# A five-pair block in Down, and a last pair that multiplies with tokens stationary onto transposed accumulators

## The chip, the cores and the metric

The kernel runs on one core of one Trainium2 chip. The metric is the device time of one execution, in microseconds (us). Five engines work side by side and wait for each other through semaphores: TensorE (PE; PEld is its weight load), VectorE (DVE), ScalarE (ACT), GpSimd (POOL) and SyncE (SP), whose queue starts most of the DMAs. Matmul results go to PSUM, which has eight banks of 128 partitions by 512 fp32 values; DVE and ACT read them from there.

## The reference

One step of a transformer layer over 576 tokens that matter to the output (512 prompt rows and 64 sample rows) with 2048 features. After attention, the part that the change touches is:

```python
h = rmsnorm(x, lp['norm_ffn_g'])
x = x + (jax.nn.silu(h @ lp['ffn_w_gate']) * (h @ lp['ffn_w_up'])) @ lp['ffn_w_down']
...
y_prompt = rmsnorm(xp[:, N_META:], final_norm_g)
y_sample = rmsnorm(xs, final_norm_g)
```

The hidden width is 5632, so that Down (`@ ffn_w_down`) sums over 44 rows of 128 hidden features, taken as 22 pairs. `rmsnorm` divides each token by the root of the mean of its squared features and multiplies each feature by its gain.

## The kernel before

All activations lie transposed: features on partitions, tokens along the free dimension (576 tokens, in two halves of `QH` = 288). Every fp32 value is split in two fp32r parts, a high one (copied by ACT) and a low one (the rest, subtracted by DVE, L157 and L154), and a product is three matmuls: high by high, high by low, low by high.

Gate, up and most of Down run as a scheme of seven products instead of eight (`winograd`): two 128-row blocks of weights and two token halves make a 2 by 2 problem; sums and differences of the weight quarters are formed on POOL and DVE (L1220), those of the token quarters once per pair (`G.tensor_tensor` at the end of each gate-and-up turn), and each of the seven results is added into up to two quarters.

The gate-and-up loop goes over `u` = 0 to 21. At its end pair `u` of the hidden activations is spilled to DRAM (`opspill`) by `spill_operands`, whose steps are taken one at a time between the products of the following turns: first the four plain quarters as high and low part, then, for pairs that Down takes in seven products, the four differences as well. The high parts pass through one staging tile, tag `s`, with a single buffer (`squad`).

Down takes the pairs in blocks: `blocks = [4, 4, 4, 4, 4, 2]`. In each of the first five, for each of eight groups of 256 output columns (`d`), `down_rows` loads 1024 rows of weights (`fetch_raw`, two buffers, requested ahead), splits them product by product and runs 7 products of 12 matmuls with 288 columns (weights stationary, tokens streaming, lines L1234 and L1238). DVE adds each product into the accumulators `y[0..15]` in SBUF (L1500). Operands of the next block are loaded by `builder`, one per product (`step`). Each pair has one of eight slots, `m % 8`: seven tiles `b1_s` to `b7_s`.

The last block, pairs 20 and 21, is plain: `plain_rows` runs 24 matmuls for each token half and column group, loading and splitting the weights once for each half. `squares` then squares each y half on POOL or ACT, sums over column groups on POOL (L1521, L1524), and multiplies y by the final gain on ACT (L1525). `finish(h)` sums over partitions with small matmuls against ones (L1552), forms the reciprocal root (`rsqrt`, L166 to L170), turns y into token rows by transposes on PE (L1538), scales them on the way out of PSUM (L1568, L1570) and stores them. `finish` of the first half is interleaved with the second half's matmuls.

The program is written as one order; the compiler places each engine's instructions by readiness and by that order, except where `keep_in_program_order` binds them. Each engine and the SP queue then run what they have in strict order.

Of the kernel before, what the change touches and what calls it, by code (L numbers as in the profile page):

```python
# [116 lines left out]
def encoder_step(  # L117
# [32 lines left out]
    def f32(ap):  # L150
        return ap.bitcast(F32)
# [167 lines left out]
    with ExitStack() as ph:  # L319
# [223 lines left out]

        rows = 39
        gT = cp.tile([P, rows], F32, name="gT")
        gF, gE, gq, gkv, g08 = (gT[:, a:b] for a, b in ((0, 16), (16, 32), (32, 36), (36, 38), (38, 39)))

# [86 lines left out]
        def projections():  # L634
# [20 lines left out]
            def bias_table():  # L655
# [8 lines left out]
                row = 0  # L664
                for g in (g_ffn, g_fin, g_q, g_kv, g_sub):
# [687 lines left out]

    def builder(m0, count, plain, by_product=False):

        places = {1: 0, 2: 1, 4: 2, 5: 3} if plain else {1: 0, 2: 2, 3: 3, 5: 4, 6: 5, 4: 6, 7: 7}
        todo = [(m, p) for m in range(m0, m0 + count) for p in places]
        if by_product:
            order = [p for p, _ in CHAIN]
            todo.sort(key=lambda mp: order.index(mp[1]))  # L1360
        for m, p in todo:
            hl = bc.tile([P, 2, QH], F32R, name=f"b{p}_{m % 8}")
            load(f32(hl), opspill[m, :, places[p]])
            operands[m % 8, p] = hl[:, 0], hl[:, 1]
            yield

    def spill_operands(m, parts):
# [26 lines left out]

    blocks = [4, 4, 4, 4, 4, 2]

# [17 lines left out]
    start = builder(0, blocks[0], False, True)  # L1414
    for u in range(FC // 2):
# [56 lines left out]

    def plain_rows(m0, n, d, hs, slots, done):

        banks = {(f, h): pmt()[:, 0:QH] for f in range(2) for h in hs}
        r = fetched.pop((m0, d, hs))
        for g in range(0, n, 2):
            wh = fw.tile([P, 2, 4, P], F32R, name="wh", tag="wh", bufs=2)
            wl = fw.tile([P, 2, 4, P], F32R, name="wl", tag="wl", bufs=2)
            for f in range(2):  # L1480
                split(wh[:, f], wl[:, f], r[:, 2 * g:2 * g + 4, f * P:(f + 1) * P])
                for k in range(4):
                    m = slots[g + k // 2]
                    ops = [operands[m, ((1, 2), (4, 5))[k % 2][h]] for h in hs]
                    mm3([banks[f, h] for h in hs], wh[:, f, k], wl[:, f, k], [o[0] for o in ops],
                        [o[1] for o in ops], g + k == 0, g + k == n + 1)
        for f in range(2):
            for h in hs:
                c = y[2 * d + f][:, h * QH:(h + 1) * QH]
                V.tensor_tensor(c, c, banks[f, h], op=ALU.add)  # L1490
                done(2 * d + f, h)

    def down_rows(m0, n, d, slots, step):
# [10 lines left out]

    tok = [[(0, NS), (NS, P), (192, 96)], [(QH, P), (416, P), (544, 32)]]
    sqs = {}
    LATE = 2
    s4 = squad()

    def squares(i, h):  # L1510
        c = y[i][:, h * QH:(h + 1) * QH]
        if h and i >= KC - LATE:
            sqs[h, i] = s4[:, 2 + i % 2]
            S.activation(sqs[h, i], c, AF.Square)
        elif i == 0:
            sqs[h] = s4[:, h]
            G.tensor_tensor(sqs[h], c, c, op=ALU.mult)
        else:
            t = s4[:, 2 + i % 2]
            if h or i % 2 == 0:  # L1520
                G.tensor_tensor(t, c, c, op=ALU.mult)  # L1521
            else:
                S.activation(t, c, AF.Square)  # L1523
            G.tensor_tensor(sqs[h], sqs[h], t, op=ALU.add)  # L1524
        S.activation(c, c, AF.Copy, scale=gE[:, i:i + 1])  # L1525

    def finish(h, ahead):

        groups = [(q, j) for q in range(4) for j in range(3)]

        def turned(q, j):
            o, n = tok[h][j]
            ps = pmt()
            for k in range(4):
                PE.transpose(ps[0:n, k * P:(k + 1) * P], y[q * 4 + k][:, o:o + n], ident)  # L1538
            return ps

        held = []
        for g in groups[:ahead]:
            held.append(turned(*g))
            yield
        pc = pmt()
        vc = yy.tile([P, 3], F32, name=f"vc{h}")
        rc = yy.tile([P, 3], F32, name=f"rc{h}")
        V.memset(vc, 1.0)
        for j, (o, n) in enumerate(tok[h]):
            parts = [sqs[h]] + [sqs[h, i] for i in range(KC - LATE, KC) if h]  # L1550
            for q in parts:
                PE.matmul(pc[0:n, 2 * j:2 * j + 2], q[:, o - h * QH:o - h * QH + n], ones[:, 0:2],  # L1552
                          start=q is parts[0], stop=q is parts[-1])
            V.tensor_scalar(vc[0:n, j:j + 1], pc[0:n, 2 * j:2 * j + 1], 1.0 / D, EPS, op0=ALU.mult, op1=ALU.add)
        rsqrt(rc, vc)
        yield
        for i, (q, j) in enumerate(groups):
            o, n = tok[h][j]
            ps = held.pop(0) if held else turned(q, j)
            k = i - i // 3  # L1560
            if h and i % 3 < 2:
                if k % 4 == 0:
                    four = fd.tile([P, 4, 512], F32, name="ot", tag="raw", bufs=2)
                ot = four[:, k % 4]
            else:
                ot = yy.tile([P, 4, P], F32, name="ot", tag="ws", bufs=3).rearrange("p a b -> p (a b)")
            if i % 2:
                S.activation(ot[0:n], ps[0:n, :], AF.Copy, scale=rc[0:n, j:j + 1])  # L1568
            else:
                V.tensor_scalar(ot[0:n], ps[0:n, :], rc[0:n, j:j + 1], None, op0=ALU.mult)  # L1570
            cs = slice(q * 512, (q + 1) * 512)
            out_queue = G.dma_start if h and i in (1, 3, 4, 7) else store
            if o == 0:
                out_queue(y_sample[:, cs], ot[0:NS])
            else:
                out_queue(y_prompt[o - NS:o - NS + n, cs], ot[0:n])
            yield

    wanted, m0 = [], 0
    for bi, n in enumerate(blocks):  # L1580
        last = bi + 1 == len(blocks)
        wanted += [(m0, d, (h,)) for h in range(2) for d in range(KC // 2)] if last else [(m0, d) for d in range(KC // 2)]
        m0 += n
# [3 lines left out]
    def fetch_raw():  # L1587
        if wanted:
            key = wanted.pop(0)
            fetched[key] = load_raw(fd, w_down, key[0] * 256, 2 * sizes[key[0]], key[1] * 256, 2)  # L1590

    fetch_raw()
    for _ in start:
        pass
    first = 0
    for bi, n in enumerate(blocks):
        slots = [(first + k) % 8 for k in range(n)]
        if bi + 1 < len(blocks):
            build = builder(first + n, blocks[bi + 1], bi + 2 == len(blocks))

# [5 lines left out]
            for d in range(KC // 2):  # L1606
                if bi == 0 and d + 1 < KC // 2:
                    load_y(d + 1)
                down_rows(first, n, d, slots, step)
                fetch_raw()  # L1610
                if bi + d == 0:
                    for _ in spilling:
                        pass
                    close_rw()
                    yy, close_yy = pool("yy", "right")
            for _ in build:
                pass
        else:
            before = iter(())
            tc.keep_in_program_order(S.preload_act_table_set("natural_log_exp_and_others"))  # L1620
            for h in range(2):
                for d in range(KC // 2):
                    plain_rows(first, n, d, (h,), slots, squares)
                    fetch_raw()
                    for _ in range(min(d, 2)):
                        next(before, None)
                before = finish(h, 5 * h)
            for _ in before:
                pass
        first += n  # L1630
    close_yy()
    close_fd()
    close_fc()
# [68 lines left out]
```

## Time and profile before

| | us |
|---|---|
| median of 3 runs (lowest, highest) | 2421.4 (2421.13, 2422.16) |
| span of the profiled execution | 2421.5 |
| attention and projections | to about 888 |
| gate and up | about 888 to 1879 |
| Down, five blocks of seven products | about 1879 to 2340.3 |
| two plain pairs, norm, output | 2340.3 to 2421.5 |

The profiled execution's own time lies among the three runs; its span is within 0.1 us of their median. In the profile a group of instructions is named by its line, its engine and what it writes from what. Busy time of PE includes overlap of matmuls in flight, so the price of a matmul is read from start to start of its successors, not from its duration. Windows give the busy time of each engine in a stretch, then the granted clock of PE (PEclk), the busy share of the DMA engines, and GB/s.

### The profile page before, as it was taken

To read this page: it belongs to the slowest core of one execution; us is meant where nothing else is said; L and a number is where in the kernel's file an instruction comes from. 1 tells how busy PE (TensorE), PEld (TensorE's weight loads), DVE (VectorE), ACT (ScalarE), POOL (GpSimd) and SP (SyncE) were. 2 spreads that over 40 slices of the span, in tenths; PEclk is the share of its full clock that TensorE was granted. 3 is DMA by queue.
4 is the path that set the end of the run, shared out by engine and by line. 5 is a ranking of instruction groups with operands and counts; after the bars stand their busy time and mean duration, and the time that the engine had idled before them with its cause. 6 is when DMAs were issued, how large, how long until landed. Compare 5 with 4: busy or idle time off the path is not lost. (4 is left out here: it accounts for less than half of the span.)

```text
span 2421.5 us, 44043 instructions
## 1 busy us (share of the span) xinstructions
PE 2362.1 (98%) x17472; PEld 2324.8 (96%) x17472; DVE 1897.9 (78%) x2781; ACT 1134.4 (47%) x2005; POOL 778.4 (32%) x514
## 2 busy tenths in 40 slices
PE   7999999999999999999999999999999999999998
PEld 6999999999998999999999999999999999999997
DVE  5666677676674789888888888898887888888875
ACT  5445555444443554444444444444444433333345
POOL 1100000130000456554554654555554222222235
PEclk9999999999999999999999999999999999999999
DMA  7433333253323643445444444544446873663434
GB/s 220 141 100 88 91 86 95 73 172 103 114 89 127 183 147 130 134 145 164 141 140 156 157 130 149 164 133 142 161 153 222 304 259 111 217 219 102 135 105 149
DMA packets 362886, 354.21 MB, mean 146 GB/s; under 512 B 23970, under 2 KB 320568, under 8 KB 362680
## 3 DMA queue, kind: packets, MB, share of 16 engines
q1 hardware_dynamic: 360694, 345.76, 45.4%
q0 software_dynamic: 1648, 5.12, 0.7%
q8 instruction: 137, 2.24, 0.4%
q14 instruction: 69, 0.57, 0.1%
q10 hardware_dynamic: 338, 0.52, 0.1%
HBM read 271.09 MB, written 81.16 MB: 145 GB/s over the span
## 5 line engine op out<-in xcount | busy, mean ns | idle before, releaser
L1234 PE MATMUL m<-b,wh 128*128 128x288 f32 x7168 | 1046.2, 295 | 1.9 <-ACT wh L157 1.9
L1234 PEld LDWEIGHTS m<-b,wh 128*128 128x128 f32 x7168 | 982.8, 188 | 3.2 <-ACT wh L157 2.7
L1238 PE MATMUL m<-b,wl 128*128 128x288 f32 x3584 | 582.8, 298 | 6.3 <-DVE wl L154 3.0
L154 DVE TENSOR_TENSOR wl<-raw,wh 128x1024 fp32r<-128x1024 f32 (+1 forms) x379 | 530.8, 1404 | 55.3 <-ACT wh L157 55.0
L1238 PEld LDWEIGHTS m<-b,wl 128*128 128x128 f32 x3584 | 511.4, 188 | 16.3 <-DVE wl L154 16.2
L157 ACT ACTIVATE wh<-raw 128x1024 fp32r<-128x1024 f32 (+1 forms) x379 | 329.7, 874 | 377.9 <-PE m L1234 326.3
L1220 POOL TENSOR_TENSOR ws<-raw 128x512 f32<-128x512 f32 (+1 forms) x124 | 219.7, 1772 | 607.2 <-DVE wl L154 351.8
L157 ACT ACTIVATE wh<-ws 128x512 fp32r<-128x512 f32 (+1 forms) x248 | 193.4, 780 | 280.2 <-DVE wl L154 118.8
L154 DVE TENSOR_TENSOR wl<-ws,wh 128x512 fp32r<-128x512 f32 (+1 forms) x248 | 247.4, 998 | 5.1 <-ACT wh L157 4.6
L109 PE MATMUL ps<-xh,wh 128*128 128x296 f32 (+1 forms) x992 | 223.6, 307 | 2.1 <-DVE ls L586 1.2
L109 PE MATMUL ps<-xl,wh 128*128 128x296 f32 (+1 forms) x992 | 215.9, 299 | 0.5 <-DVE xl L162 0.5
L109 PE MATMUL ps<-xh,wl 128*128 128x296 f32 (+1 forms) x960 | 208.0, 298 | 0.0
L1374 DVE TENSOR_TENSOR c<-c,s 128x288 fp32r<-128x288 f32 x168 | 166.4, 990 | 0.0
L109 PEld LDWEIGHTS ps<-xh,wh 128*128 128x128 f32 x992 | 160.6, 190 | 4.7 <-ACT wh L157 1.4
L109 PEld LDWEIGHTS ps<-xl,wh 128*128 128x128 f32 x992 | 161.5, 190 | 0.9 <-DVE xl L162 0.9
L1500 DVE TENSOR_TENSOR y<-y,m 128x288 f32<-128x288 f32 x280 | 125.7, 449 | 40.9 <-PE m L1238 40.8
L109 PEld LDWEIGHTS ps<-xh,wl 128*128 128x128 f32 x960 | 156.1, 190 | 0.0
L1220 POOL TENSOR_TENSOR raw<-raw 128x1024 f32<-128x1024 f32 (+1 forms) x46 | 143.2, 3113 | 3.5
L157 ACT ACTIVATE wh<-wr 128x1024 fp32r<-128x1024 f32 (+1 forms) x110 | 101.7, 924 | 88.2 <-PE ps L109 59.5
L1330 DVE TENSOR_TENSOR c<-c,m 128x288 f32<-128x288 f32 x171 | 73.2, 449 | 88.7 <-PE m L1238 51.5
L154 DVE TENSOR_TENSOR wl<-wr,wh 128x1024 fp32r<-128x1024 f32 (+1 forms) x108 | 116.0, 1074 | 28.0 <-ACT wh L157 25.9
L1393 POOL TENSOR_TENSOR c<-c,rb 128x576 f32<-128x576 f32 x44 | 79.0, 1795 | 139.2 <-ACT c L1392 139.2
(368 smaller groups left out, 3164.3 us busy)
## 6 DMA issues: line engine op xcount, KB each, us to landing
raw<-in_ffn_w_gate SPq DMA_DIRECT2D x44, 1024.0 KB, 9.2
raw<-in_ffn_w_up SPq DMA_DIRECT2D x44, 1024.0 KB, 6.9
b<-opspill SPq DMA_DIRECT2D x148, 288.0 KB, 6.0
raw<-in_ffn_w_down SPq DMA_DIRECT2D x40, 1024.0 KB, 5.7
wr<-in_w_in SPq DMA_DIRECT2D x57, 512.0 KB, 4.0
opspill<-s SPq DMA_DIRECT2D x42, 576.0 KB, 3.1
opspill<-c SPq DMA_DIRECT2D x42, 576.0 KB, 6.3
wr<-in_w_out SPq DMA_DIRECT2D x16, 512.0 KB, 4.3
```

Of the source, the lines that this page charges most:

```text
L109: self.tc.keep_in_program_order(self.pe.matmul(out, lhsT, rhs, start=start, stop=stop))
L154: V.tensor_tensor(lo, src, f32(hi), op=ALU.subtract)
L157: S.activation(hi, src, AF.Copy)
L1220: (G if p in (5, 7) else V).tensor_tensor(x, y, z, op=ALU.add if p == 5 else ALU.subtract)
L1234: PE.matmul(banks[p], wh[:, k, :], x, start=first and new and k == 0 and x is hi, stop=False, skip_group_check=not new)
L1238: PE.matmul(banks[p], wl[:, k, :], hi, start=False, stop=last and k == n - 1, skip_group_check=not new)
L1330: V.tensor_tensor(c, c, banks[p], op=ALU.add)
L1374: V.tensor_tensor(src[:, k].bitcast(F32R), src[:, k], f32(hi[:, k]), op=ALU.subtract))
L1393: G.tensor_tensor(g[:, f, :], g[:, f, :], rb2, op=ALU.mult)
L1500: V.tensor_tensor(c, c, banks[p], op=ALU.add)
```

## The change

`blocks` becomes `[4, 4, 4, 4, 5, 1]`.

The fifth block takes five pairs in seven products (15 matmuls a product). Pair 20 is therefore spilled with its differences (the test `u < FC // 2 - blocks[-1]` now lets it through). Its seven operands share slot 4 with pair 12 of the fourth block; `builder` asks for them in the fourth block's last column group, one behind each product. A load of weight rows has up to 1280 rows; its two buffers become one in each of two pools (`fd`, `fe`). Two of the accumulators, y13 and y14, move to the buffer of tag `s`.

The last pair, 21, runs the other way round. `last_operands` loads its plain quarters as four tiles of 576 tokens and its 256 rows of weights as eight tiles of 512 columns, and splits these, all during the fifth block and into slots 5 to 7. `last_rows` then goes over five token tiles (four of 128 prompt tokens, one of 64 sample tokens) and four groups of 512 columns: four transposes lay y into a bank as token rows, and six matmuls (two hidden blocks by three parts, tokens stationary, 512 weight columns streaming) add the last pair onto it. ACT squares the bank with a sum along the row and copies it out; the reciprocal root is formed per token tile; DVE multiplies by it and by the gain, which is loaded as rows on all partitions; the tile is stored. The transposed gain `gE`, `plain_rows`, `squares` and `finish` go.

```diff
-        rows = 39
+        rows = 23
...
-    blocks = [4, 4, 4, 4, 4, 2]
+    blocks = [4, 4, 4, 4, 5, 1]
...
+        if count > 4:
+            for _ in range(49 - len(todo)):
+                yield
+            for p in order:
+                fetch_operand(m0 + 4, p)
+                yield
...
-            y.update((i, yy.tile([P, TQ], F32, name=f"y{i}")) for i in range(13, KC))
+            y2 = fr.tile([P, 2, TQ], F32, name="y", tag="s", bufs=1)
+            y[13], y[14] = y2[:, 0], y2[:, 1]
+            y[15] = yy.tile([P, TQ], F32, name="y15")
...
+    def last_operands():
+
+        for f in range(2):
+            for s in range(2):
+                t = bc.tile([P, 2, QH], F32R, name="lt", tag=spare.pop(0))
+                load(f32(t), opspill[last_m, :, 2 * f:2 * f + 2, s])
+                tokens[f, s] = t.rearrange("p a b -> p (a b)")
+                yield
+        raws = {}
+        for c in range(4):
+            for f in range(2):
+                raws[f, c] = bc.tile([P, 512], F32, name="lr", tag=spare[2 * c + f])
+                r0 = (2 * last_m + f) * P
+                load(raws[f, c], w_down[r0:r0 + P, c * 512:(c + 1) * 512])
+                yield
+        turn = spare[8:] + spare[:8]
+        for c in range(4):
+            for f in range(2):
+                hi, lo = (bc.tile([P, 512], F32R, name=n, tag=turn.pop(0)) for n in ("lh", "ll"))
+                split(hi, lo, raws[f, c])
+                w_last[f, c] = hi, lo
+                yield
+                yield
...
+            for c in range(4):
+                bank = pmt()[0:n]
+                for k in range(4):
+                    PE.matmul(bank[:, k * P:(k + 1) * P], y[4 * c + k][:, o:o + n], ident, is_transpose=True,
+                              start=k == 0, stop=False)
+                for f in range(2):
+                    for t, s in ((0, 0), (1, 0), (0, 1)):
+                        PE.matmul(bank, tokens[f, t][:, o:o + n], w_last[f, c][s], start=False,
+                                  stop=f == 1 and s == 1)
+                x, junk = chunk("lx"), chunk("lj")
+                S.activation(junk[0:n], bank, AF.Square, accum_out=ssq[0:n, c:c + 1])
+                S.activation(x[0:n], bank, AF.Copy)
+                if final:
+                    V.tensor_tensor(x[0:n], x[0:n], gains[c][0:n], op=ALU.mult)
+                xs.append(x)
+            v = yy.tile([P, 1], F32, name="v", bufs=2)
+            r = yy.tile([P, 1], F32, name="r", bufs=2)
+            V.reduce_sum(v[0:n], ssq[0:n], axis=AX.X)
+            V.tensor_scalar(v[0:n], v[0:n], 1.0 / D, EPS, op0=ALU.mult, op1=ALU.add)
+            rsqrt(r[0:n], v[0:n])
+            for c, x in enumerate(xs):
+                cs = slice(c * 512, (c + 1) * 512)
+                if not final:
+                    V.scalar_tensor_tensor(x, x, r, gains[c], op0=ALU.mult, op1=ALU.mult)
+                    store(rows[:, cs], x)
+                elif c < 2:
+                    V.tensor_scalar(x[0:n], x[0:n], r[0:n], None, op0=ALU.mult)
+                    store(rows[:, cs], x[0:n])
+                else:
+                    S.activation(x[0:n], x[0:n], AF.Copy, scale=r[0:n])
+                    S.dma_start(rows[:, cs], x[0:n])
...
-            build = builder(first + n, blocks[bi + 1], bi + 2 == len(blocks))
+            build = last_operands() if bi + 2 == len(blocks) else builder(first + n, blocks[bi + 1])
...
+                    other, close_other = pool("fe")
+                    into.insert(0, other)
+                fetch_raw()
```

More of the change, by code (lines that the diff above doesn't have):

```diff
@@ L1471, in encoder_step @@
     fd, close_fd = pool("fd")
[L1473 to L1491, printed above, removed]
     def down_rows(m0, n, d, slots, step):
@@ L1527, in finish @@
[L1527 to L1577, printed above, removed]
@@ L1579, in encoder_step @@
     wanted, m0 = [], 0
-    for bi, n in enumerate(blocks):
-        last = bi + 1 == len(blocks)
-        wanted += [(m0, d, (h,)) for h in range(2) for d in range(KC // 2)] if last else [(m0, d) for d in range(KC // 2)]
+    for n in blocks[:-1]:
+        wanted += [(m0, d) for d in range(KC // 2)]
         m0 += n
@@ L1618, in encoder_step @@
         else:
-            before = iter(())
             tc.keep_in_program_order(S.preload_act_table_set("natural_log_exp_and_others"))
[L1621 to L1629, printed above, removed]
+            last_rows()
         first += n
     close_yy()
+    close_other()
     close_fd()
```

65 lines of the change are left out of this document (33 added, 32 removed).

## The prediction

> **What bounds the kernel now.** I read the page first, then the busy times by stage, then the order of PE's instructions in Down and at the end.
>
> ```profile
> PE 2362.1 (98%) x17472; PEld 2324.8 (96%) x17472; DVE 1897.9 (78%) x2781; ACT 1134.4 (47%) x2005; POOL 778.4 (32%) x514
> ```
>
> ```profile
> core 0: us, PE busy (x) PEld busy (x) DVE busy (x) ACT busy (x) POOL busy (x), PEclk, DMA share, GB/s
> ...
> 1859.20:1880.70 21.50, 21.50 (x164) 21.50 (x163) 11.87 (x13) 8.48 (x14) 8.58 (x6) 1.00 1.06 387
> 1880.70:1900.00 19.30, 17.66 (x129) 16.99 (x129) 17.91 (x34) 8.14 (x14) 4.73 (x4) 1.00 1.03 341
> 2248.70:2340.30 91.60, 91.04 (x674) 89.48 (x674) 80.19 (x129) 36.73 (x58) 18.63 (x14) 1.00 0.31 95
> 2340.30:2380.10 39.80, 36.58 (x256) 33.86 (x255) 23.46 (x46) 24.68 (x50) 24.69 (x30) 1.00 0.49 155
> 2380.10:2404.00 23.90, 23.90 (x177) 23.86 (x178) 18.43 (x29) 12.88 (x26) 16.45 (x21) 0.93 0.46 142
> 2404.00:2421.50 17.50, 8.29 (x76) 7.16 (x73) 6.18 (x14) 6.17 (x13) 2.20 (x4) 0.89 0.51 169
> ```
>
> TensorE is the bound nearly everywhere, so a change counts by the PE time that it removes, plus what it does to the few stretches where PE waits. The fifth Down block lasts from 2248.7 to 2340.3. Behind it stand 81.2 us (to 2421.5): the two plain pairs with the turned output between them, and a drain in which PE is busy for 8.3 of 17.5 us. All that is replaced lies in these last two stretches; the two rows ahead of them are the entry into Down, where the change adds a spill.
>
> **Price of a matmul.** The timeline at the end of the fifth block:
>
> ```profile
> 2338.18 0.70 PE L1238 MATMUL m<-b,wl 128*128 128x288 f32 x4
> 2338.72 1.22 PE L1234 MATMUL m<-b,wh 128*128 128x288 f32 x8
> 2339.77 0.70 PE L1238 MATMUL m<-b,wl 128*128 128x288 f32 x4
> ```
>
> Twelve matmuls of 288 columns from 2338.18 to 2339.77: 0.1328 us each, start to start. The new last pair streams 512 columns instead; the nearest rows stand in the attention:
>
> ```profile
> 613.43 0.40 PE L109 MATMUL po<-pk0l,vh 128*128 128x512 f32 x1
> 613.67 0.40 PE L109 MATMUL po<-pk0h,vl 128*128 128x512 f32 x1
> 613.90 0.34 PE L109 MATMUL sp<-kmh,qnh 128*128 128x400 f32 x1
> ```
>
> That is 0.24 and 0.23, so 0.235 us each. The Trainium skill, page "TensorE: Matmul & The Clock Gate", section "Back-to-back issue gap", gives N/2.4 + 2.5 ns for a lone stream, 216 ns at 512 columns; by it the 120 matmuls below would take 25.9 us instead of 28.2. The rows here, each with its own weight load, are slower, and I go by them.
>
> The chain of waits gives the transposes and the present end:
>
> ```profile
> 2400.08 0.87 PE m L1538 x8
> 2400.96 3.18 PE m L185 x24
> 2404.14 3.06 PE m L1538 x28
> ...
> 2409.68 0.21 ACT rc L166
> ...
> 2411.41 0.74 DVE ot L1570
> ...
> 2414.99 0.68 ACT ot L1568
> ```
>
> A transpose costs 0.109 us (28 in 3.06, 8 in 0.87), and going from matmuls to transposes and back costs nothing beside (0.87 and then 3.18 for 24 at 0.1325).
>
> **The change, part by part.**
>
> *The fifth block with five pairs.* It had 8 x 84 = 672 matmuls, 89.2 us; it lasts 91.6, so 2.4 us are stalls, about 0.3 at each of the seven changes of columns. It gets 8 x 105 = 840 matmuls, 111.6 us. I keep the 2.4 us (0 at best, 1.25 times at worst): 114.0, ending at 2362.7. DVE decides whether more is lost:
>
> ```profile
> L154 DVE TENSOR_TENSOR wl<-raw,wh 128x512 fp32r<-128x512 f32 x22 | 22.2, 1007 | 0.0
> L1500 DVE TENSOR_TENSOR y<-y,m 128x288 f32<-128x288 f32 x49 | 22.0, 449 | 6.8 <-PE m L1238 6.8
> ```
>
> Of DVE's 80.2 us in the block, 56 additions into y take 25.1 and stay the same; the other 55.1 grow by 5/4. That is 94.0 us of 114. The last pair's eight splits, which move into this block, add 8 x 1.0 = 8, still 12 us under PE. But they are asked for within three columns (43 us), where DVE then has 35.3 + 8: full. Price between 0 and about 4 us (half of the splits uncovered); I take 0, because the splits are needed only after the block and the products' own splits stand ahead of them.
>
> *Fetching the fifth pair.* Its seven operands go into slot 4, which the fourth block still reads in its last columns; each can be loaded only after its product. The plain pairs load into slots 4 and 5 at the same border now:
>
> ```profile
> 2238.60 5.65 SPq L138 DMA_DIRECT2D b<-opspill  x6
> 2248.16 0.38 SPq L138 DMA_DIRECT2D raw<-in_ffn_w_down  x1
> ```
>
> ```profile
> b<-opspill SPq DMA_DIRECT2D x148, 288.0 KB, 6.0
> ```
>
> Columns take 11.5 us (91.6/8), so the loads start 1.4 us into the last columns, right after the first product, and 10 us ahead of the border at 2248.7. One lands after 6 us and is wanted 1.1 us past the border at the earliest (eight matmuls of the other four pairs): it costs nothing. Each load holds SP for about 0.9 us (5.65/6); behind it stand weight rows for the columns after the next, with 14 us of room, and the last pair's own loads, wanted 100 us later.
>
> *The last pair.* It removes 384 matmuls (51.0 us), 96 transposes (10.5), 24 sums of squares over partitions, 16 loads of 512 KB, 32 splits, and the gain and square of each y. It adds per bank 4 transposes and 6 matmuls of 512 columns: 0.436 + 1.41 = 1.85 us; 20 banks (five token tiles by four column groups) 36.9 us, since 64 tokens stationary stream as many columns as 128. The handover inside a bank, matmuls adding onto a transposed block, stands nowhere in the trace; between nothing (the row above, for other banks) and 20 x 0.16 us, a transpose's 273 ns less its 0.109, that is 3.3 us. I take nothing, by the nearer row. ACT must empty a bank in less than 1.85 us:
>
> ```profile
> L393 ACT ACTIVATE junk<-xn 128x512 f32<-128x512 f32 x8 | 5.0, 624 | 0.1
> ...
> L393 ACT ACTIVATION_READ_ACCUMULATOR junk<-xn 128x1 f32 x8 | 1.5, 189 | 0.0
> ```
>
> Square 0.62, its read 0.19 and a copy out of the bank 0.68 (the row at 2414.99) make 1.49 us; with logarithm and exponential 6.4 us a tile against PE's 7.4. DVE has four products by gain (0.74 each) and five small steps: about 4. Both hide behind PE; DVE's last additions into y hide behind the first three banks. The four broadcast loads of the gain go out in the fifth block's last columns and are wanted 7 us into the last pair; a tile's stores leave while the next one is multiplied. The weight rows keep two buffers, now one in each of two pools, and y13 and y14 only move to another buffer: nothing. So PE ends at 2362.7 + 36.9 = 2399.6.
>
> *The drain.* Behind the last matmul: its latency over its slot 0.17, ACT 1.49, product by gain 0.74, sum and mean 0.4, the five norm steps 1.1 (at 0.21 each, by the first at 2409.68), two scalings on DVE 1.5 beside two on ACT, and the stores:
>
> ```profile
> out<-ot SPq DMA_DIRECT2D x4, 128.0 KB, 2.6
> ```
>
> 2.6 us, and about 1.2 behind the last landing (an estimate: SP's last store now starts at 2417.4, takes 2 to 2.9, and the span ends at 2421.5). Together 9.2, so 2408.8.
>
> *Pair 20's differences.* It is now a seven-product pair: four POOL subtractions, four ACT copies, four DVE subtractions and two 576 KB stores more, in the last gate-and-up turn, where DMA is full (387 GB/s):
>
> ```profile
> 1827.86 0.37 SPq L141 DMA_DIRECT2D opspill<-s  x1
> ...
> 1877.40 0.44 ACT L1372 ACTIVATE s<-c 128x288 fp32r<-128x288 f32 x1 [2.82 <-POOL c L1457]
> ```
>
> The regular place of this store is one pair of turns (2 x 168 matmuls, 44.6 us) behind 1827.86: 1872.5. The staging tile s has one buffer, so pair 21's copy, now at 1877.40, has to wait for that landing, at 6 us or more until 1878.5 to 1881; queued behind it on ACT are the copies of Down's first weights, and PE already stands idle for 1.6 us in the stretch from 1880.7 to 1900. The 1.18 MB also push the 28 operand loads back by 3 us. Between 0 and 6 us; I take 1.2, near the lower end, because PE's present wait there already holds the weights back by as much.
>
> **Sum:** 2408.8 + 1.2 = 2410.0. It is made against the span of 2421.5; the median of the runs is 2421.4, so I shift nothing: 2410, 11.4 us less.
>
> **Rivals.** (a) *The entry into Down* takes its full 6 us (ACT held, then DMA): 2414.7. For: DMA at 1.06, one buffer. Against: the compiled order may put pair 21's copy later.
> (b) *The fifth pair comes late*: its seven loads stand behind the weight-row load that waits for the end of the block before. The first is then issued as the block starts, lands at 6 us and is wanted at 1.1: 5 us, and the clock after it costs 1.3 more (below): 2416. For: SP does wait at such loads. Against: six of the eight go ahead of it at 2238.60.
> (c) *DVE becomes the fifth block's bound*: 4 us for splits, 3.3 for the handover or growing stalls: about 2417.
> (d) *It goes better*: stalls vanish, as DVE falls from 88% to 82%, the entry costs nothing, the drain is shorter: 2404 to 2406.
> (e) *Slower: the clock.* PE's clock halves in the last pair.
>
> ```profile
> 2380.10 0.48 PE L1552 MATMUL m<-ones,s 128*96 128x2 f32 x2 [1.41 <-DVE vc L1554]
> ...
> 2380.83 0.44 PE L185 MATMUL m<-b,wl 128*128 128x288 f32 x1
> 2381.07 0.68 PE L185 MATMUL m<-b,wh 128*128 128x288 f32 x2
> ```
>
> After 1.41 us idle, in a stretch thinned by tiny matmuls, 288 columns took 0.24 us instead of 0.133 for about 2.8 us (the granted clock of that stretch is 0.93). If ACT or the banks make PE wait at every tile, 120 matmuls at 0.43 and 80 transposes at up to 0.22 need 60 to 69 us, 24 to 32 more: 2434 to 2442. It decides once each tile holds a gap of some 1.5 us. Against it: ACT's 6.4 of 7.4 us, eight banks, and 8 transposes in every 4.05 us (2400.08) that left the clock at full. The Trainium skill, page "TensorE: Matmul & The Clock Gate", section "Part 4: PE-mode transpose", says that transposes do not count as PE-busy for this gate, which speaks for it; by that rule 24% of the last pair would look idle, and the trace with 21% shows no drop.
>
> **Chances.** Forecast (2407 to 2413) 0.58; (a) 0.08; (b) 0.08; (c) 0.10; (d) 0.10; (e) 0.06. A measurement of this kernel tells about 0.2%, 4.8 us, from no change: faster is below 2416.6. Forecast, (a), (d), most of (b) and a third of (c) are there: 0.84. The rest of (b) and (c), the same: 0.10. (e): slower 0.06. The range reaches from (d) to (c): 2403.5 to 2417.5; it leaves out (e) and tails.
>
> **What would show it.** Fifth block about 114 us with PE over 97% busy; no PE wait on a DMA of b at its start; 512-column matmuls 0.235 apart and banks 1.85; PE's end 9 us before the span's end; PE's wait near 1881 up from 2 to 3 us. Wrong would be: a first product of the fifth block held for more than 2 us, PE idle between banks, a granted clock under 0.95 before the drain, or banks of 2 us and more.

## The result and the profile after

The changed kernel takes 2406.84 us (median of 4 runs, 2403.98 to 2408.42) against 2421.78 for the kernel before: a ratio of 0.9931, 95% interval 0.9919 to 0.9943. The forecast was 2410. Its sign was right and its sum 3 us too high. Inside the sum, an entry into Down that costs more than was taken is outweighed by two gains that the prediction does not have at all. One execution of the run before_shifted below took 3352 us at a granted clock of 0.63; it is left out of that kernel's row.

The busy times by stage of the changed kernel (columns as in the prediction: stretch, its length, busy time of PE, its weight loads, DVE, ACT and POOL, granted clock, DMA share, GB/s). The stretches are the two of the entry into Down, the fifth block, the last pair, and the drain:

```profile
core 0: us, PE busy (x) PEld busy (x) DVE busy (x) ACT busy (x) POOL busy (x), PEclk, DMA share, GB/s
1859.20:1880.70 21.50, 21.28 (x160) 20.92 (x158) 14.49 (x17) 9.40 (x16) 8.31 (x5) 1.00 0.97 351
1880.70:1900.00 19.30, 15.83 (x108) 14.45 (x108) 16.02 (x27) 7.40 (x15) 4.00 (x3) 1.00 1.03 352
2246.36:2359.10 112.74, 111.61 (x843) 111.31 (x841) 92.44 (x135) 45.57 (x64) 24.28 (x14) 1.00 0.35 116
2359.10:2395.70 36.60, 36.60 (x202) 29.02 (x200) 16.20 (x40) 23.64 (x65) 0.00 (x0) 1.00 0.31 115
2395.70:2404.30 8.60, 0.15 (x1) 0.00 (x0) 2.48 (x9) 2.82 (x7) 0.00 (x0) 0.70 0.30 62
```

The fifth block has its 840 matmuls (three records of its neighbours fall into the stretch) in 112.74 us; DVE is busy 82% of it. The last pair keeps PE busy without a hole, at full clock. The entry into Down lost 1.8 us of PE time against the same window before (15.83 busy against 17.66). The border between block and last pair, in PE's order:

```profile
2358.43 0.83 PE L1238 MATMUL m<-b,wl 128*128 128x288 f32 x5
2359.10 0.60 PE L1546 MATMUL m<-ident,y 128*128 128x128 f32 x4
2359.45 0.71 PE L1550 MATMUL m<-lh,lt 128*128 128x512 f32 x2
2360.00 0.40 PE L1550 MATMUL m<-ll,lt 128*128 128x512 f32 x1
2360.24 0.62 PE L1550 MATMUL m<-lh,lt 128*128 128x512 f32 x2
2360.69 0.40 PE L1550 MATMUL m<-ll,lt 128*128 128x512 f32 x1
2360.93 0.27 PE L1546 MATMUL m<-ident,y 128*128 128x128 f32 x1
```

Four transposes and six matmuls from 2359.10 to 2360.93: 1.83 us a bank, 512 columns 0.23 to 0.24 apart, and nothing lost between the transposes and the matmuls that add onto them. The drain from 2395.7 on takes 8.6 us.

Read against the forecast on the span (2410.0): the fifth block begins at 2246.36 instead of 2249.9 (-3.5), takes 112.7 instead of 114.0 (-1.3), the last pair 36.6 instead of 36.9 (-0.3), the drain 8.6 instead of 9.2 (-0.6); together -5.7, the span of 2404.3. The largest part lies ahead of all that the change was thought to touch. So most experiments went there.

### The profile page after: what moved, and what is told of

Same layout as the page of the kernel before. It is cut to its first block, busy times and chain, and to the rows that moved or that the text cites. A ratio compares the mean times of both kernels' runs of the same rounds, so it can differ in the third digit from the quotient of the medians.

```text
span 2404.3 us, 43647 instructions
## 1 busy us (share of the span) xinstructions
PE 2344.6 (98%) x17336; PEld 2305.3 (96%) x17336; DVE 1886.0 (78%) x2750; ACT 1127.8 (47%) x1999; POOL 740.7 (31%) x463
## 5 line engine op out<-in xcount | busy, mean ns | idle before, releaser
L1234 PE MATMUL m<-b,wh 128*128 128x288 f32 x7280 | 1061.6, 294 | 6.2 <-ACT wh L157 2.9
L1234 PEld LDWEIGHTS m<-b,wh 128*128 128x128 f32 x7280 | 995.4, 188 | 9.0 <-ACT wh L157 4.9
L154 DVE TENSOR_TENSOR wl<-raw,wh 128x1024 fp32r<-128x1024 f32 (+2 forms) x347 | 509.5, 1469 | 40.7 <-ACT wh L157 40.3
L157 ACT ACTIVATE wh<-raw 128x1024 fp32r<-128x1024 f32 (+2 forms) x347 | 313.6, 904 | 367.2 <-PE m L1234 320.1
L1220 POOL TENSOR_TENSOR ws<-raw 128x512 f32<-128x512 f32 (+2 forms) x124 | 224.9, 1814 | 615.3 <-DVE wl L154 361.2
L157 ACT ACTIVATE wh<-ws 128x512 fp32r<-128x512 f32 (+2 forms) x248 | 196.6, 793 | 284.9 <-PE m L1234 113.6
L154 DVE TENSOR_TENSOR wl<-ws,wh 128x512 fp32r<-128x512 f32 (+2 forms) x248 | 250.1, 1008 | 7.7 <-PE m L1238 4.4
L1384 DVE TENSOR_TENSOR c<-c,s 128x288 fp32r<-128x288 f32 x172 | 170.8, 993 | 0.0
```

The lines of the kernel that those rows point to most:

```text
L154: V.tensor_tensor(lo, src, f32(hi), op=ALU.subtract)
L157: S.activation(hi, src, AF.Copy)
L1220: (G if p in (5, 7) else V).tensor_tensor(x, y, z, op=ALU.add if p == 5 else ALU.subtract)
L1234: PE.matmul(banks[p], wh[:, k, :], x, start=first and new and k == 0 and x is hi, stop=False, skip_group_check=not new)
L1384: V.tensor_tensor(src[:, k].bitcast(F32R), src[:, k], f32(hi[:, k]), op=ALU.subtract))
```

## The experiments

Each was timed against the kernel before on the same chip. The stage lengths are read from PE's timeline of one profiled execution each: *gate and up* from the first matmul of L1234 to the first of Down, *blocks 1-4* from there to the first product of the fifth block, *fifth* to the first matmul behind it.

| kernel | us | ratio, interval | gate and up | blocks 1-4 | fifth |
|---|---|---|---|---|---|
| before | 2421.8 | | 989.25 | 370.79 | 91.51 |
| changed | 2406.8 | 0.9931 (0.9919-0.9943) | 986.28 | 368.88 | 112.74 |
| five_pairs_plain_last | 2435.9 | 1.0055 (1.0042-1.0067) | 989.57 | 376.50 | 110.70 |
| one_bank | 2434.0 | 1.0043 (1.0030-1.0055) | 987.01 | 369.58 | 112.70 |
| no_pair20_differences | 2402.4 | 0.9917 (0.9903-0.9930) | 985.82 | 366.22 | 112.70 |
| staging_free | 2407.2 | 0.9935 (0.9922-0.9947) | 986.46 | 371.73 | 112.99 |
| splits_spread | 2406.5 | 0.9935 (0.9922-0.9949) | 986.45 | 369.94 | 112.64 |
| splits_bound | 2406.3 | 0.9927 (0.9915-0.9940) | 985.95 | 370.15 | 111.26 |
| buffers_alone | 2422.8 | 1.0004 (0.9996-1.0013) | 989.16 | 371.01 | 91.79 |
| before_shifted | 2420.0 | 0.9982 (0.9973-0.9991) | 982.69 | 370.25 | 91.32 |
| after_shifted | 2410.7 | 0.9945 (0.9931-0.9958) | 989.56 | 370.89 | 112.58 |
| sums_shifted | 2425.9 | 1.0011 (1.0002-1.0020) | 989.57 | 372.48 | 91.59 |
| best_addresses | 2400.2 | 0.9908 (0.9895-0.9922) | 983.19 | 370.82 | 110.89 |
| y_behind_operands | 2403.7 | 0.9920 (0.9906-0.9933) | 982.29 | 374.03 | 110.70 |

### What the turned last pair is worth: five_pairs_plain_last

```diff
-    blocks = [4, 4, 4, 4, 4, 2]
+    blocks = [4, 4, 4, 4, 5, 1]
...
-                split(wh[:, f], wl[:, f], r[:, 2 * g:2 * g + 4, f * P:(f + 1) * P])
-                for k in range(4):
+                split(wh[:, f, 0:2], wl[:, f, 0:2], r[:, 0:2, f * P:(f + 1) * P])
+                for k in range(2):
```

(on the kernel before, with the changed kernel's buffers and operand loads)

> The five-pair block, the moved buffers and pair 20's differences as in the changed kernel, but the last pair run as before (24 matmuls of 288 columns become 12 for each half and column group; squares, transposes and output as before). Theory: the block itself is worth little, the turned last pair nearly everything. 168 matmuls more and 192 fewer at 0.1328 us are -3.2 us; the entry into Down costs 3.1 more and the columns of blocks one to four 2.7 less, as in the changed kernel: 2421.8 - 2.8 = about 2419. Rival, the block is worth as much as the turned pair: 2414 or less.

Measured 2435.9 us: slower than before by 13 us (0.42 to 0.67%), where 2419 was expected, and 29 us slower than the changed kernel. The fifth block is not it (110.7 us). Blocks 1-4 take 5.7 us longer than before, 4.8 of it in the first two column groups (see the entry, below). The larger part lies behind the fifth block, in PE's last stretch:

```profile
2365.14:2428.20 63.06, 51.85 (x314) 44.71 (x312) 41.00 (x86) 36.37 (x87) 40.29 (x53) 0.86 0.32 102
```

By price that is 192 matmuls (25.5 us) and 96 transposes (10.5 us), 36 us in all, as much as the turned pair's 36.6. It took 63. Waits of that stretch (who waited for whom, us in total, times, longest) and PE's order in it:

```profile
ACT y L1546 <- POOL sq L1542: 16.8, 18, 2.2
PEld m L185 <- ACT wh L157: 9.0, 9, 2.7
```

```profile
2390.01 0.29 PE L185 MATMUL m<-b,wl 128*128 128x288 f32 x1
2392.79 0.77 PE L185 MATMUL m<-b,wh 128*128 128x288 f32 x3 [2.48 <-ACT wh L157]
...
2395.32 0.68 PE L185 MATMUL m<-b,wh 128*128 128x288 f32 x2
2395.80 0.44 PE L185 MATMUL m<-b,wl 128*128 128x288 f32 x1
```

With one pair, a bank has 6 matmuls (0.8 us) where it had 12, but ACT and POOL have as much to do per column group as before: the squares, the sums and the gain. ACT's gain multiplication waits for POOL's square, the copy of the next weights stands behind it on ACT, and PE waits for that copy. Then the clock goes too: 288 columns from 2395.32 to 2395.80 are 0.24 us apart, and the granted clock of the stretch is 0.86. So the two halves of the change are not independent parts that add up: the five-pair block with the old last pair loses, and what the turned pair buys is not fewer PE cycles but that its 36 us can be fed. Its weights are split ahead of time, and ACT has two instructions per 1.83 us bank. Whether a plain last pair with its weights split ahead would do as well was not tried.

### The clock rival: one_bank

```diff
+        whole = pmt()
         for j, (o, n) in enumerate(places):
...
-                bank = pmt()[0:n]
+                bank = whole[0:n]
```

> The changed kernel with a single bank for the whole last pair, so that PE waits at each of the 20 token-and-column blocks until ACT has squared and copied the one before (about 1.5 us of idle in every 3.4). It measures the clock rival of the prediction. If the granted clock stays at full: 19 x 1.5 us more, 2435. If such gaps halve it: 120 matmuls and 80 transposes cost another 20 to 30 us, 2455 to 2465, with 512-column matmuls at 0.43 instead of 0.23 us.

Measured 2434.0, as the first case says. The stretch of the last pair in windows, and two banks in PE's order:

```profile
2360.22:2425.10 64.88, 40.84 (x202) 27.55 (x200) 16.53 (x40) 23.61 (x65) 0.00 (x0) 1.00 0.18 65
```

```profile
2361.36 0.62 PE L1551 MATMUL m<-lh,lt 128*128 128x512 f32 x2
2361.82 0.40 PE L1551 MATMUL m<-ll,lt 128*128 128x512 f32 x1
2363.48 0.66 PE L1547 MATMUL m<-ident,y 128*128 128x128 f32 x4 [1.27 <-ACT lx L1555]
```

PE idles 1.25 to 1.27 us at each of the nineteen changes of bank, is busy for 63% of 65 us, and the clock stays at 1.00, with 512 columns at 0.23 (2361.36 to 2361.82 for two). So rival (e) of the prediction would not have come about even with gaps of 1.27 us at every bank. The Trainium skill, page "TensorE: Matmul & The Clock Gate", section "Why this matters for your kernels", asks for no idle gap over about 3 us; this run agrees, and it does not bear out for this mix the rule that the prediction cited on transposes. The run five_pairs_plain_last does not fit so simply: there 288 columns took 0.24 us instead of 0.133 after gaps of 2.5 us and less. What tells the two apart, the length of single gaps or the share of small ones, these runs don't settle.

### The entry into Down: no_pair20_differences, staging_free

```diff
-        if u < FC // 2 - blocks[-1]:
+        if u < FC // 2 - 2:
...
-        load(f32(hl), opspill[m, :, PLACES[p]])
+        load(f32(hl), opspill[19 if m == 20 and PLACES[p] > 3 else m, :, PLACES[p]])
```

> The changed kernel with pair 20's four differences neither formed nor spilled; Down reads pair 19's in their place, with the same loads (this part of the result is then not what the reference computes). Theory: the staging tile and the two added stores hold ACT's copies at the entry into Down; without them the first product to the fourth takes 6.9 us again instead of 10.0, time about 2403.8. Rival, the entry is held by the operand loads on the full DMA queue or by the new order, and not by the spill: 9 to 10 us, time 2406.8.

```diff
-            store(opspill[m, :, first:first + 4, 0], f32(hi))
+            store(opspill[m, :, first:first + 4, 0], src if (m, first) == (20, 4) else f32(hi))
```

> The changed kernel with pair 20's high parts of the differences stored from the tile that then holds the low parts, not from the staging tile: the same copies, subtractions and bytes, but the staging tile need not wait for that store (this part of the result is then not what the reference computes). Without the whole spill the time was 2402.4. Theory: the staging tile with its one buffer holds pair 21's copies and with them Down's first weights; then this kernel gains the same, the first product to the fifth block takes 366 us, time 2402.5 to 2403.5. Rival: the 1.18 MB on a full DMA do it; 369 to 370 us, 2406.8.

Without the differences: 2402.4, and blocks 1-4 take 366.2 us instead of 368.9 (369.6 to 370.2 in three more executions of the changed kernel's own entry). All of it lies in the first two column groups, 168 matmuls: 25.2 us instead of 28.0, while the other thirty take 341.0 and 340.9. So the added spill costs 3 to 4 us, in the predicted range of 0 to 6, but three times the 1.2 that was taken. The reason given for it is wrong: with the staging tile freed early, nothing is gained (2407.2, 371.7 us). SP's queue shows what else moved. Before, the changed kernel, and the kernel without the differences, from the load of y0 and y1 to the last operand of Down's first block:

```profile
1836.75 0.81 SPq L138 DMA_DIRECT2D y<-x2spill  x2
...
1858.08 22.61 SPq L138 DMA_DIRECT2D b<-opspill  x28
```

```profile
1857.17 16.34 SPq L138 DMA_DIRECT2D b<-opspill  x20
1873.95 0.37 SPq L141 DMA_DIRECT2D opspill<-s  x1
1879.74 0.79 SPq L138 DMA_DIRECT2D y<-x2spill  x2
1880.63 0.38 SPq L141 DMA_DIRECT2D opspill<-c  x1
1881.11 5.62 SPq L138 DMA_DIRECT2D b<-opspill  x8
```

```profile
1835.79 0.86 SPq L138 DMA_DIRECT2D y<-x2spill  x2
...
1857.02 21.68 SPq L138 DMA_DIRECT2D b<-opspill  x28
```

The first two accumulators are loaded into a tile of the gate's tag. Before, pair 20's gate tile was free for that at 1836.75, long ahead. In the changed kernel it holds pair 20's differences until they are stored; the load goes into the other tile, which is free only when POOL has multiplied pair 21 (at 1879.7), and the compiled order puts it ahead of the last eight operand loads. SP stands at it from 1874.3 to 1879.7, and the eight loads go out at 1881 to 1887. PE's and DVE's order in the changed kernel:

```profile
1884.64 0.69 PE L1238 MATMUL m<-b,wl 128*128 128x288 f32 x4
1887.44 1.30 PE L1234 MATMUL m<-b,wh 128*128 128x288 f32 x8 [2.11 <-issue]
```

```profile
1882.98 0.45 DVE L1492 TENSOR_TENSOR y<-y,m 128x288 f32<-128x288 f32 x1
...
1886.17 0.44 DVE L1492 TENSOR_TENSOR y<-y,m 128x288 f32<-128x288 f32 x1
1886.54 0.44 DVE L1384 TENSOR_TENSOR c<-c,s 128x288 fp32r<-128x288 f32 x1
1886.90 0.44 DVE L1492 TENSOR_TENSOR y<-y,m 128x288 f32<-128x288 f32 x1
```

PE is idle for 2.11 us before Down's fifth product, and the view names nothing for it. The semaphore events in the trace do: the weight load of this product waits for DVE and for a DMA, and the last to come is DVE's at 1887.35, the end of the addition at 1886.90, which frees a bank of PSUM; the DMA's last event is at 1886.46. It is not one of the eight late operand loads that PE waits for: the third of them lands at 1888.35, when PE has begun with the product's third pair (1888.05). What is late is y. Its load lands at 1882.6 and 1883.6, the first addition begins 5.5 us behind Down's first product (3.0 in the kernel before and without the differences), and the additions then stand on DVE among pair 21's subtractions (L1384).

In other executions of the same order the clock halved behind this gap as well (splits_spread: 0.91 from 1880 to 1900): twelve matmuls of 288 columns at 0.24 us, and a first column group of 16.5 us instead of 15.0. The second column group also loses, 13.0 us against 11.1 without the differences, in several short waits for weight splits; what lies behind those was not settled.

### The eight splits: splits_spread, splits_bound

In the changed kernel the fifth block has one stall, here in DVE's and PE's order:

```profile
2256.40 2.66 DVE L154 TENSOR_TENSOR ll<-lr,lh 128x512 fp32r<-128x512 f32 x2
2256.63 1.88 POOL L1220 TENSOR_TENSOR ws<-raw 128x640 f32<-128x640 f32 x1 [2.84 <-DVE wl L154]
...
2258.99 0.44 DVE L1492 TENSOR_TENSOR y<-y,m 128x288 f32<-128x288 f32 x1
...
2259.57 0.62 PE L1234 MATMUL m<-b,wh 128*128 128x288 f32 x3 [1.13 <-DVE y L1492]
```

Two splits of the last pair take 2.66 us beside POOL's sum, an addition into y stands behind them, and PE waits for its bank. (The Trainium skill, page "SBUF — State Buffer", section "SBUF: two separate sides", says that a DVE operation with two inputs in SBUF and a GpSimd operation that reads it shut each other out; these rows agree, 1.33 us a split here against the 0.69 that one of this size took at 1881.65, with POOL idle.) First the requests alone were spread, then they were bound to the written order as well:

```diff
-                split(hi, lo, raws[f, c])
+                tc.keep_in_program_order(S.activation(hi, raws[f, c], AF.Copy))
+                tc.keep_in_program_order(V.tensor_tensor(lo, raws[f, c], f32(hi), op=ALU.subtract))
                 w_last[f, c] = hi, lo
-                yield
-                yield
+                for _ in range(5):
+                    yield
```

> The changed kernel with the last pair's eight splits asked for one in every five products of the fifth block instead of one in every two. Theory: the one stall of the fifth block, 1.29 us behind its first column, is DVE held by these splits; it goes away, the block takes 111.5 us instead of 112.7, time about 2405.5. Rival, a stall of POOL's sums against DVE at the change of columns that would be there anyway: 112.7 us, time 2406.8.

> The changed kernel with the last pair's eight splits asked for one in every five products, and bound to the written order on ACT and DVE (without that binding the order did not change at all: the run with the spread alone was the same program again). Theory: the fifth block's one stall of about 1.2 us is an addition into y that stands behind two of these splits on DVE; with them apart, the block takes 111.5 us instead of 112.7 and the time is about 2405.5. Rival: the stall is that of POOL's sum and DVE at the change of columns, and stays; 112.7 us, 2406.8.

Spread alone, the compiler put every instruction where it had been: the run repeats the changed kernel (2406.5; 112.64 us). Bound, the stall is gone and the block takes 111.26 us, PE busy throughout (111.26 in its window). So these splits cost 1.4 us, in the predicted 0 to 4, where 0 was taken. The total did not fall by it (2406.3): 1.4 us is less than the intervals leave open, and the profiled execution's entry had the halved clock.

### The pace of gate and up: buffers_alone, before_shifted, after_shifted

Gate and up are the same instructions in the same order, yet 3.0 us shorter after the change, though PE's idle time in them is no shorter (2.8 us before, 3.6 after). buffers_alone is the kernel before with two pools for the weight rows and y13 and y14 in the staging tile's place:

> The kernel before with only the buffers moved (weight rows in two pools with one buffer each, y13 and y14 in the staging tile's place); blocks and last pairs as before. Theory: the short stalls at each change of columns in blocks one to four go away through the buffers; from the fourth product of the first block to the fourth of the fifth 368.7 us become 365 to 366, time 2418.5 to 2419.5. Rival, they vary from program to program, or from execution to execution, with the order in which POOL and DVE happen to meet: 368 to 369 us, time 2421.8.

Nothing: 2422.8, 989.16 and 371.0 us. What else the change moves is where tiles lie: the transposed gains lose 16 columns, so all tiles of the left-hand pools (weight rows, their splits, the gate tiles, most of y) start 64 bytes lower. The same one-line edit was made on both kernels; no instruction moves:

```diff
-        gT = cp.tile([P, rows], F32, name="gT")
+        gT = cp.tile([P, rows + 16], F32, name="gT")[:, 0:rows]
```

> The kernel before with 16 unused columns behind the transposed gains, so that every tile of the left-hand pools lies 64 bytes further on; the same instructions in the same order on every engine. Theory: the changed kernel's 16 fewer gain columns moved these tiles by 64 bytes, and that is why its gate-and-up products take 3.18 us instead of 3.194 and its column groups lose less in DVE's stalls; then one of the two addresses is the better one, the pace becomes 3.18, blocks one to four lose 2 to 3 us, and the time is 2415 to 2417. Rival, the addresses mean nothing and the paces differ for another reason: 3.194 us, 2422.6 us.

> The changed kernel with the 16 gain columns put back unused, so that the tiles of the left-hand pools lie where they lay before; the same instructions in the same order. Theory of addresses: a gate-and-up product takes 3.194 us again, the blocks' stalls come back, time 2411 to 2413. Rival: 3.18 us and 2406.8 us.

Matmuls in 400 us without idle PE, in windows of before, after_shifted, the changed kernel, and before_shifted:

```profile
1000.00:1400.00 400.00, 400.00 (x3008) 400.00 (x3008) 344.30 (x324) 192.25 (x288) 211.99 (x108) 1.00 0.46 149
```

```profile
1000.00:1400.00 400.00, 400.00 (x3008) 400.00 (x3008) 344.45 (x324) 192.50 (x286) 211.97 (x108) 1.00 0.46 149
```

```profile
1000.00:1400.00 400.00, 400.00 (x3022) 400.00 (x3021) 346.62 (x324) 193.21 (x287) 212.67 (x109) 1.00 0.46 149
```

```profile
1000.00:1400.00 400.00, 400.00 (x3030) 400.00 (x3029) 348.17 (x325) 193.86 (x288) 213.96 (x109) 1.00 0.46 149
```

That settles it: at the addresses of before, both kernels run 3008 matmuls; 64 bytes lower 3022, 64 bytes higher 3030, which is 0.1330, 0.1324 and 0.1320 us each. In the table the five kernels at the first place take 989.2 to 989.6 us for gate and up, the six at the second 985.8 to 987.0, the three at the third 982.3 to 983.2, and each of the three groups was run on several chips. The changed kernel at the old addresses takes 2410.7 us. So some 4 of the 15 us (3.4 by the ratios, 3.9 by the medians) are owed to 16 columns of a small tile. The kernel before, shifted, does not keep all of the 6.6 us of its gate and up: it is 0.18% faster (some 4 us), and its profiled execution is 5.2 us shorter than before's, as gate and up begin at 890.7 instead of 888.8. All kernels at the second and third place begin them at 889.5 to 894.3, those at the first at 888.2 to 889.5; whether that is the addresses too was not tried.

### The columns of blocks one to four: sums_shifted

after_shifted still takes 370.9 us for blocks 1-4, no more than before, though its first two column groups take 28.1 us instead of 24.7. The other thirty take 342.8 instead of 346.1, so they lose less than before's. One suspect was the place of POOL's sums ws:

```diff
-            y.update((i, yy.tile([P, TQ], F32, name=f"y{i}")) for i in range(13, KC))
+            y.update((i, yy.tile([P, TQ + 16 * (i == 15)], F32, name=f"y{i}")[:, 0:TQ]) for i in range(13, KC))
```

> The kernel before with the tiles of the pool yy (the sums ws of Down, y13 and y14) 64 bytes lower, to the place modulo 256 bytes that ws has in the changed kernel; everything else at its address, the same instructions in the same order. Theory: the column groups of blocks one to four lose 0.3 us each less in the changed kernel because of where ws lies; then from the first Down product to the fifth block 370.8 us become 368, and the time is 2420. Rival: ws has nothing to do with it: 370.8 us, 2422.8, and the cause of that gain stays open.

The opposite: blocks 1-4 take 372.5 us and the time is 2425.9. The groups by line in 325 us of the four blocks (1905 to 2230) show where it goes, for before, the changed kernel and sums_shifted:

```profile
L1220 DVE TENSOR_TENSOR ws<-ws,raw 128x512 f32<-128x512 f32 x28 | 19.4, 693 | 15.7 <-POOL ws L1220 14.2
```

```profile
L1220 DVE TENSOR_TENSOR ws<-ws,raw 128x512 f32<-128x512 f32 x29 | 20.1, 692 | 11.3 <-POOL ws L1220 9.3
```

```profile
L1220 DVE TENSOR_TENSOR ws<-ws,raw 128x512 f32<-128x512 f32 x28 | 19.4, 693 | 21.6 <-POOL ws L1220 20.5
```

DVE waits for POOL's sum, 14.2 us in total before, 9.3 after, 20.5 here. Moving ws alone changes that wait, but not in the direction supposed. What sets it in the changed kernel (ws and the weight rows lie further apart there, since they have room for five pairs) stays open.

### Two versions for the better: best_addresses, y_behind_operands

best_addresses is splits_bound with `rows + 32` in the line of gT, so that the left-hand pools lie where before_shifted has them.

> The changed kernel with the last pair's splits apart and bound (fifth block 111.3 us) and 32 unused columns behind the transposed gains, so that the left-hand pools lie where the shifted kernel before had them (160 modulo 256 bytes). Theory: gate and up take 982.7 us instead of 986.3, the rest stays, time about 2403. Rival: with the changed kernel's other tiles this address is no better: 986 us, 2406.3.

It is the fastest: 2400.2, ratio 0.9908 (0.9895 to 0.9922), with 983.2 us of gate and up and a fifth block without a stall. To it the last run adds:

```diff
-                    if products[0] == 2:
-                        load_y(0)
                     for _ in range(blocks[0]):
                         next(start, None)
+                    if products[0] == 7:
+                        load_y(0)
```

> The kernel best_addresses with the load of the first two accumulators (y0, y1) asked for after the last product of the last gate-and-up turn instead of after its second, so that on SP's queue it stands behind all 28 operand loads of Down's first block and not ahead of the last eight. Theory: in the changed kernel pair 20's two stores moved these loads; SP is held from 1874.32 to 1879.74 by the y load, which waits until POOL has done with the tile; the last eight operand loads start 1881.11, and the fourth product's operands land at 1887.4: PE's 2.1 us of idle and the clock behind it. With the y load behind them the entry's stalls fall from 6.4 to about 2.4 us and the time from 2400.2 to 2396.5. Rival, it is pair 20's 1.18 MB on a full DMA: the same bytes still go ahead of the eight loads, 2400.

Slower by 3 us (3.5 by the medians, 2.9 by the ratios, whose intervals overlap), where 4 us less was expected. In its timeline:

```profile
1885.09 0.45 DVE L1492 TENSOR_TENSOR y<-y,m 128x288 f32<-128x288 f32 x1 [2.15 <-DMA y<-x2spill]
...
1885.59 0.61 PE L1234 MATMUL m<-b,wh 128*128 128x288 f32 x1 [6.05 <-DVE y L1492]
```

The operand loads are all out before 1879, but the y load, issued at 1879.09, 5.5 us behind Down's first product (2.3 in the changed kernel), lands when the first additions into y have long been due, and PE waits 6.05 us for a bank. The theory of this run, that PE waited for operands (of Down's fifth product, which it calls the fourth), is not borne out: with the operands early and y later, a wait for a bank grew from 2.1 to 6.05 us. That fits the order of the entry above, where y was late by less. What might help, y0 and y1 in a tile that is free early as it was before, was not tried.

## Why the prediction came out right

**Last pair.** Right: 36.6 us for 36.9, 0.23 to 0.24 us for 512 columns, no cost at the handover, clock at full, ACT well inside PE's time (busy 23.6 of the 36.6 us, where 32 were priced). Rival (e) is out by far.

**Fifth block.** 112.7 for 114.0, two errors against each other. "I keep the 2.4 us" failed: the stalls at the changes of columns did not scale, they vanished, as rival (d) had it (splits_bound: 111.26 us, less than 840 x 0.1328); no run shows why. The other mis-sized term is the splits: taken as free, they cost 1.4. Rival (c) is out: DVE has 82%, as (d) had it.

**Fetching the fifth pair.** Right as to its price. SP's queue at the border:

```profile
2235.53 1.93 SPq L138 DMA_DIRECT2D b<-opspill  x2
...
2245.74 0.38 SPq L138 DMA_DIRECT2D raw<-in_ffn_w_down  x1
2246.22 1.08 SPq L138 DMA_DIRECT2D b<-opspill  x2
```

The last two of the seven do stand behind the weight rows, as rival (b) feared, but they belong to late products; PE does not wait for any.

**Entry.** The term was mis-sized (1.2 taken, 3 to 4 measured), and its mechanism is wrong. Its sign came true (PE's idle time near 1881 up from 1.6 to 2.9 us), but for another reason. The prediction looked for who needs the staging tile, and for operand loads that are pushed back; in this trace no operand load ends a wait of PE there. What moved is the next tenant of the *other* tile that the differences occupy: the accumulators' first load goes out 43 us later, and PE waits for the bank of an addition into them. The prediction counted the DMAs that the step adds, not those that its buffer pushes aside.

**The start of the fifth block.** The prediction kept the old 2248.7, to which the entry's 1.2 comes. This step failed most: 3.5 us too late in spite of the dearer entry. Addresses give 3.0 us in gate and up; attention took 2.4 longer in this execution; in blocks 1-4 the first two column groups took 3.3 us more than before, and the other thirty 5.2 less. In after_shifted these thirty gain only 3.3, so some 2 of the 5.2 go with the addresses; the rest stays open. No row of the old profile shows that a pace depends on where a tile lies, so this could not have been read from it; that tiles move could.

**Between span and time** every run here has about 2 us (1.75 to 2.20). So the page of before, with a span of 2421.5, shows an execution of about 2423.5 by estimate, above the runs listed at the front and not among them. "I shift nothing" came out right only since that execution lay, by this estimate, 1.7 us above the median, nearly as far as a span lies below its time; that was luck.

With the old addresses the changed kernel takes 2410.7 us, the forecast's 2410 almost exactly. That closeness is in part luck too: there the first two column groups of Down take 3.3 us more than before (1.2 was taken), and the other thirty 3.3 us less (nothing was taken). What the prediction had right by its reasoning is the last pair, the fetch of the fifth pair and, but for its small terms, the fifth block.

## What to carry to other kernels

When a step keeps a buffer longer, look for the next tenant of that buffer and where its load then stands on its queue: here the moved load delayed the additions that free PE's banks, while no load of the added bytes was seen to end a wait of PE (a part of the loss stays open). When work per bank is halved, ask whether the engines that feed and empty the bank are halved too; the same 36 us of matmuls took 63 where they were not. And before a few tenths of a per cent are put down to an edit, shift the tiles by 64 bytes and see what that does alone.

## What the runs showed of the hardware

A stream of matmuls with 288 columns that never waits ran at 0.1330, 0.1324 or 0.1320 us each, with nothing changed but the start of the left-hand tiles by 64 bytes at a time. Which of the moved tiles matters, and whether PE's reads meet those of other engines, the runs don't show.

Nineteen gaps of 1.27 us in 65 us left PE's clock at full, while elsewhere one gap of 2.1 us before Down's fifth product was followed by twelve matmuls at 0.24 us instead of 0.132 in some executions (splits_spread) and by none in others of the same order (the changed kernel).
